# Moving the residual's multiplications by gamma from GpSimd to VectorE in a two-layer transformer trunk

## The chip, the cores and the metric

The kernel runs on one core of a Trainium2 chip. The metric is the device time of one execution in microseconds (us). A core has a matrix engine (TensorE, PE in the profile; its loads of stationary operands are PEld), VectorE (DVE), ScalarE (ACT), GpSimd (POOL) and SyncE (SP), which issues DMAs. Each engine works through its own list of instructions in order, and waits at an instruction until what it needs is there.

## The reference

The trunk has two layers over 256 tokens with 2048 channels, in float32. Layer 0 mixes tokens by gated linear attention (GLA), layer 1 by a neighbourhood attention (16 heads), and each mixer is followed by a gated feed-forward block of 5632 channels with a convolution of width 3 ("FFN"). Behind each of the four sub-layers stands

```
x = layer_norm(alpha * x + f(x), gamma, beta)
# layer_norm: (x - mean) * rsqrt(var + 1e-5) * gamma + beta, over the 2048 channels
```

so there are four normalizations: behind GLA, FFN 0, attention and FFN 1. The first three ("mid") feed another sub-layer, the last gives the output.

## The kernel before

**Matmuls.** float32 is emulated: each operand x is split into `hi` (a rounded copy, ScalarE, line 131) and `lo` = x - `hi` (VectorE, line 132), and three products hi·hi, hi·lo, lo·hi are added in PSUM. The weights (416 units of 1 MB) come by DMA into `raw`, are split in two halves each, and wait in four pairs of buffers. So VectorE makes two `lo` halves of 128x1024 for every unit, all through the program.

**Layout.** The residual stream lies in `x_sb`, two tiles of 128 tokens (t = 0, 1) by 2048 channels. The activations that feed the matmuls are held transposed and split, in `xT` (input of a sub-layer) and `gT` (its inner result). A sub-layer's last matmul (`residual_out`) gives blocks of 128x512; VectorE adds them into `x_sb` (lines 365, 367) and takes statistics (line 371). For the last block, t = 0 is finished first and then t = 1, and the next sub-layer's first block of matmuls is written the same way ("apart"): 48 matmuls (16 chunks of channels, three products each) that read `xT` of t = 0, then 48 that read t = 1.

**A mid normalization** (`ln_mid`, line 287) is, for each t:
- head: mean and variance (`ln_mv`, line 282); variance + epsilon (`rs_m`, line 274) and its power -1/2 (`ln_rs`, line 275), both on GpSimd; then four 128x512 pieces (x - mean)·rstd in place on VectorE (line 293);
- turn, four times: four TensorE transposes of a 512-wide block of `x_sb` (line 299) into one of three PSUM buffers `ps_tp`; gamma and beta per channel by ScalarE (line 307) and VectorE (line 309) in turns; then the split into `xT` (lines 131, 132);
- resid (line 312): `x_sb` itself, for the next residual sum, is multiplied by gamma in four 128x512 pieces on GpSimd (line 315, gamma in the tile `g`, copied to all partitions), and beta is added by an accumulating DMA (line 316).

**Order.** The code is written in the order of PE's work. Small steps are put into a list (`later`) with a due time in "ticks" (a tick is called every few matmuls). The order on each engine that results is not the written order: a scheduler places instructions by priority (written order, shifted by offsets for the splits and the turns) and by when it expects their inputs.

**Pools.** `gb`, the tile of gamma, lies in the pool of the stage (ffn0, ffn1). In the attention stage the tiles `bt` (bias, loaded by two GpSimd DMAs at lines 706 and 707), `qk` and `pt` have two buffers each.

Of the kernel before, what the change touches and what calls it, by code (L numbers as in the profile page):

```python
# [17 lines left out]
P = 128  # L18
# [58 lines left out]
def kernel(  # L77
# [92 lines left out]

    side = []

# [98 lines left out]
    def rsqrt(dst, src, scale, eps, small):  # L271

        m = small.tile([P, 1], F32, tag="rs_m", name="rs_m", bufs=2)
        nc.gpsimd.tensor_scalar(m, src, scale, eps, ALU.mult, ALU.add)  # L274
        nc.gpsimd.tensor_tensor(dst, m, mhalf, ALU.pow)  # L275
# [11 lines left out]
    def ln_mid(pool, xs, t, stats, idx, gb):  # L287
# [23 lines left out]

        def resid():
            for b in range(4):
                sl = slice(b * 512, b * 512 + 512)
                nc.gpsimd.tensor_tensor(xs[:, t, sl], xs[:, t, sl], gb[:, sl], ALU.mult)
            nc.gpsimd.dma_start(xs[:, t], lnp[idx, 1:2, :].broadcast_to([P, D]), accum_op=ALU.add)

        later(head, 0)
        for b, n in enumerate((4, 0, 0, 0)):
            later(lambda b=b: turn(b), n)  # L320
        later(resid, 0)

    def ln_last(pool, xs, t, stats, gb):
        def go():
            mv, rstd = ln_head(pool, xs, t, stats)
            nmr = pool.tile([P, 1], F32, tag="ln_nm", name="ln_nm", bufs=2)
            nc.vector.scalar_tensor_tensor(nmr, mv[:, 0:1], -1.0, rstd, ALU.mult, ALU.mult)
            for b in (3, 0, 1, 2):
                sl = slice(b * 512, b * 512 + 512)
                blk = xs[:, t, sl]  # L330
                if b == 3:
                    nc.scalar.activation(blk, blk, AF.Identity, bias=nmr, scale=rstd)
                    nc.gpsimd.tensor_tensor(blk, blk, gb[:, 0, sl], ALU.mult)
                    nc.gpsimd.tensor_tensor(blk, blk, gb[:, 1, sl], ALU.add)
                else:
                    nc.vector.scalar_tensor_tensor(blk, blk, mv[:, 0:1], gb[:, 0, sl], ALU.subtract, ALU.mult)  # L336
                    nc.vector.scalar_tensor_tensor(blk, blk, rstd, gb[:, 1, sl], ALU.mult, ALU.add)  # L337
                (nc.scalar if b == 3 else nc.sync).dma_start(out[t * P:t * P + P, sl], blk)
        later(go, 0)
# [6 lines left out]
    def load_gb(pool, idx):  # L346
        gb = pool.tile([P, 2, D], F32, tag="gb", name="gb")
        for i in range(2):
            nc.gpsimd.dma_start(gb[:, i], lnp[idx, i:i + 1, :].broadcast_to([P, D]))
        return gb  # L350

    def residual_out(act_in, first, last, n, idx, begin=None):
# [3 lines left out]
        for nb in range(4):  # L356
            def evac(t, ps):
                if begin is not None and not cell:
                    begin()
                    cell["begun"] = True  # L360
                pool, xs, gb = scope["pool"], scope["x"], scope["gb"]
                sl = slice(nb * 512, nb * 512 + 512)
                blk = xs[:, t, sl]
                if first:
                    nc.vector.scalar_tensor_tensor(blk, blk, ALPHA, ps, ALU.mult, ALU.add)  # L365
                else:
                    nc.vector.tensor_tensor(blk, ps, blk, ALU.add)  # L367
                if last:
                    if t not in stats:
                        stats[t] = pool.tile([P, 4, 6], F32, tag="ln_st", name="ln_st", bufs=2)  # L370
                    nc.vector.bn_stats(stats[t][:, nb], blk)  # L371
                    if nb == 3:
                        if idx == 2 * DEPTH - 1:
                            ln_last(pool, xs, t, stats[t], gb)
                        else:
                            ln_mid(pool, xs, t, stats[t], idx, gb)
            as_block(act_in, n, evac, apart=last and nb == 3, settle=nb == 0)
# [250 lines left out]
    def ffn(layer):  # L628
# [23 lines left out]
        for part, (c0, n) in enumerate(THIRDS):  # L652
# [39 lines left out]
            if part == 0:  # L692
                scope["gb"] = (load_gb if idx == 2 * DEPTH - 1 else load_g)(pool, idx)
            residual_out(gT, part == 0, part == len(THIRDS) - 1, n // 4, idx)


    def attention():
# [3 lines left out]
        def head(h):  # L701
            pool = scope["pool"]
            q = pool.tile([P, 2, T], F32R, tag="q", name="q", bufs=2)
            k = pool.tile([P, 2, T], F32R, tag="k", name="k", bufs=2)
            bt = pool.tile([P, 6, GW], F32, tag="bt", name="bt", bufs=2)
            nc.gpsimd.dma_start(bt, bias[h])
# [3 lines left out]
            def qk_out(dst, ps):  # L710
                f = pool.tile([P, T], F32, tag="qk", name="qk", bufs=2)
                join(pool, f, ps)
# [29 lines left out]
            def turn():  # L742
                s = cell["s"]
                tp = ps_tp()
                for kt in range(2):
                    for i in range(2):
                        nc.tensor.transpose(tp[:, kt * T + i * P:kt * T + i * P + P],
                                            s[:, i, kt * P:kt * P + P], ident)
                pt = pool.tile([P, 2, 512], F32R, tag="pt", name="pt", bufs=2)
                cell["pt"] = pt.rearrange("p h (k n) -> p h k n", k=2)  # L750
# [33 lines left out]
    def begin_gla_out():  # L784
# [5 lines left out]
        nc.gpsimd.dma_start(scope["x"], x.rearrange("(t p) d -> p t d", p=P))  # L790
        scope["gb"] = load_g(open_pool("ffn0"), 0)

    def begin_na_out():
        scope["gb"] = load_g(swap_pool("ffn1"), 2)

# [79 lines left out]
```

## Time and profile before

| what | value |
|---|---|
| median of three runs | 2297.3 us (2296.99 to 2300.06) |
| the profiled execution's own time | 2300.88 us |
| its span, first to last instruction | 2299.2 us |
| PE busy | 2265.1 us (99%) |
| VectorE busy | 1511.0 us (66%) |
| ScalarE busy | 1053.2 us (46%) |
| GpSimd busy | 371.1 us (16%) |
| line 315, the 24 multiplications on GpSimd | 44.4 us |

The busy time of an engine is an average over all stages. An engine with a share of 99% can still be held up in a few places, and an engine with 66% can be the one that is waited for in one stretch. The profiled execution took 3.6 us more than the median.

### The profile page before, as it was taken

The page shows a single profiled execution, that of the slowest core. Times are in us where ns is not written, and L with a number is a line of the kernel's source. Part 1 is how long each engine was busy: PE and PEld are TensorE (multiplying, and loading weights), DVE is VectorE, ACT ScalarE, POOL GpSimd, SP SyncE. Part 2 cuts the span into 40 slices and gives each one's busy share as a digit, 9 for nine tenths or more (in the row PEclk, how much of TensorE's full clock was granted, in tenths as well). Part 3 has the DMA queues.
Part 4 walks back from the last instruction along what each step waited for, and adds up shares of the span by engine and source line. Part 5 has one row for each costly group of instructions (what it writes and reads, how often), then busy time and mean ns, then how long its engine had stood idle before and what let it go on. Part 6 is the DMA issues. An engine that isn't in the chain of part 4 may idle for free. (4 is left out here: it accounts for less than half of the span.)

```text
span 2299.2 us, 29601 instructions
## 1 busy us (share of the span) xinstructions
PE 2265.1 (99%) x11728; PEld 1923.9 (84%) x11728; DVE 1511.0 (66%) x2053; ACT 1053.2 (46%) x1529; POOL 371.1 (16%) x312
## 2 busy tenths in 40 slices
PE   8999999999999999999999999999999999999997
PEld 7888888788888888888778888878888888888886
DVE  6656656867656675576676666667776567656775
ACT  6554543544434444344355555445444344434442
POOL 1111001222102220122120000022220022201211
PEclk9999999999999999999999999999999999999999
DMA  7444464644555556555585555556556555555452
GB/s 277 174 177 167 181 241 151 235 183 182 206 197 181 176 177 217 183 184 183 183 241 189 193 185 194 197 169 236 182 182 220 185 182 183 183 211 190 176 193 92
DMA packets 66604, 439.03 MB, mean 191 GB/s; under 512 B 7649, under 2 KB 9697, under 8 KB 15137
## 3 DMA queue, kind: packets, MB, share of 16 engines
q1 hardware_dynamic: 60336, 415.00, 50.3%
q0 software_dynamic: 5840, 21.61, 3.7%
q8 instruction: 92, 1.51, 0.3%
q10 hardware_dynamic: 288, 0.52, 0.1%
q14 instruction: 48, 0.39, 0.0%
HBM read 431.87 MB, written 2.10 MB: 189 GB/s over the span
## 5 line engine op out<-in xcount | busy, mean ns | idle before, releaser
L132 DVE TENSOR_TENSOR lo<-raw,hi 128x1024 fp32r<-128x1024 f32 (+1 forms) x793 | 950.6, 1217 | 502.1 <-ACT hi L131 500.8
L190 PE MATMUL ps_mm<-xT,hi 128*128 128x512 f32 x3472 | 1232.6, 399 | 6.4 <-ACT hi L131 6.1
L131 ACT CAST hi<-raw 128x1024 fp32r<-128x1024 f32 (+1 forms) x793 | 807.9, 1040 | 526.8 <-PE ps_mm L190 480.4
L190 PE MATMUL ps_mm<-xT,lo 128*128 128x256 f32 x3472 | 976.5, 281 | 0.3 <-DVE lo L132 0.3
L190 PEld LDWEIGHTS ps_mm<-xT,hi 128*128 128x128 f32 x3472 | 653.4, 188 | 167.2 <-ACT hi L131 6.1
L190 PEld LDWEIGHTS ps_mm<-xT,lo 128*128 128x128 f32 x3472 | 657.1, 189 | 2.1 <-DVE lo L132 1.5
L190 PE MATMUL ps_mm<-hi,gT 128*128 128x512 f32 x1920 | 594.7, 389 | 0.0
L190 PEld LDWEIGHTS ps_mm<-hi,gT 128*128 128x128 f32 x1920 | 360.4, 188 | 75.0
L647 POOL TENSOR_SCALAR c<-h,cw,cb 128x256 f32<-128x256 f32 x168 | 239.9, 1428 | 1101.6 <-DVE h L466 1101.6
L190 PE MATMUL ps_mm<-lo,gT 128*128 128x512 f32 x960 | 373.8, 389 | 0.0
L190 PE MATMUL ps_mm<-hi,xT 128*128 128x512 f32 x896 | 286.0, 393 | 1.7 <-DVE xT L132 1.7
L190 PEld LDWEIGHTS ps_mm<-lo,gT 128*128 128x128 f32 x960 | 180.2, 188 | 36.8
L190 PEld LDWEIGHTS ps_mm<-hi,xT 128*128 128x128 f32 x896 | 168.1, 188 | 37.7 <-DVE xT L132 3.5
L190 PE MATMUL ps_mm<-lo,xT 128*128 128x512 f32 x448 | 175.2, 391 | 2.9 <-DVE lo L132 2.9
L131 ACT CAST gT<-gg 128x256 fp32r<-128x256 f32 x88 | 35.6, 407 | 288.5 <-DVE gg L665 288.5
L660 ACT ACTIVATE ge<-c 128x256 f32<-128x256 f32 x88 | 36.8, 418 | 253.4 <-DVE c L649 253.4
L648 DVE SCALAR_TENSOR_TENSOR c<-h,cw,c 128x255 f32<-128x255 f32 x168 | 81.3, 484 | 76.8 <-POOL c L647 76.8
L190 PEld LDWEIGHTS ps_mm<-lo,xT 128*128 128x128 f32 x448 | 84.4, 189 | 20.9 <-DVE lo L132 4.4
L649 DVE SCALAR_TENSOR_TENSOR c<-h,cw,c 128x255 f32<-128x255 f32 x168 | 81.3, 484 | 5.9
L465 ACT COPY join_t<-ps_mm 128x256 f32<-128x256 f32 x216 | 78.3, 363 | 0.0
L466 DVE TENSOR_TENSOR h<-ps_mm,join_t 128x256 f32<-128x256 f32 x168 | 70.2, 418 | 0.0
L132 DVE TENSOR_TENSOR gT<-gg,gT 128x256 fp32r<-128x256 f32 x88 | 37.7, 430 | 38.8 <-ACT gT L131 38.8
(132 smaller groups left out, 818.8 us busy)
## 6 DMA issues: line engine op xcount, KB each, us to landing
raw<-in_w_dram SPq DMA_DIRECT2D x388, 1024.0 KB, 4.8
x_sb<-in_lnp_dram POOLq DMA_DIRECT2D x6, 1024.0 KB, 9.9
raw<-in_w_dram SPq DMA_DIRECT2D x16, 256.0 KB, 5.5
g<-in_lnp_dram POOLq DMA_DIRECT2D x3, 1024.0 KB, 13.6
bt<-in_bias_dram POOLq DMA_DIRECT2D x16, 192.0 KB, 2.8
bt<-bmask_sb POOLq DMA_DIRECT2D x16, 192.0 KB, 3.0
xr<-in_xt_dram SPq DMA_DIRECT2D x8, 256.0 KB, 5.6
x_sb<-in_x_dram POOLq DMA_DIRECT2D x1, 2048.0 KB, 9.6
```

The lines of the kernel that those rows point to most:

```text
L131: nc.scalar.copy(hi, src)
L132: nc.vector.tensor_tensor(lo, src, hi.bitcast(F32), ALU.subtract)
L190: nc.tensor.matmul(o, l, r, start=start, stop=stop)
L465: nc.scalar.copy(tmp, ps4[:, :, 1])
L466: nc.vector.tensor_tensor(dst.rearrange("p (t n) -> p t n", t=2), ps4[:, :, 0], tmp, ALU.add)
L647: nc.gpsimd.tensor_scalar(c, hh, w_[:, 1:2], cb[:, ch:ch + 1], ALU.mult, ALU.add)
L648: nc.vector.scalar_tensor_tensor(c[:, 1:], hh[:, :T - 1], w_[:, 0:1], c[:, 1:], ALU.mult, ALU.add)
L649: nc.vector.scalar_tensor_tensor(c[:, :T - 1], hh[:, 1:], w_[:, 2:3], c[:, :T - 1], ALU.mult, ALU.add)
L660: nc.scalar.activation(ge, c, AF.Gelu)
```

## The change

1. `resid` is cut into four steps, one for each 512-wide piece, that multiply on VectorE. They go into a new list `slow`, with due times 36, 44, 52 and 60 ticks behind the normalization's end; a tick takes at most one of them. The accumulating DMA stays on GpSimd's queue, behind the fourth piece.
2. `rs_m` (variance plus epsilon) goes from GpSimd to VectorE, in all the normalizations, GLA's included; the power stays on GpSimd.
3. Gamma's tile goes into the pool of `x_sb`, which lives to the end, and `load_gb` for the last normalization takes gamma from there and beta from a tile `b` of its own.
4. `bt`, `qk` and `pt` in the attention stage have one buffer in place of two.

```diff
-    side = []
+    side, slow = [], []
...
         while side and side[0][0] <= st["tick"]:
             side.pop(0)[1]()
+
+        if slow and slow[0][0] <= st["tick"]:
+            slow.pop(0)[1]()
...
         m = small.tile([P, 1], F32, tag="rs_m", name="rs_m", bufs=2)
-        nc.gpsimd.tensor_scalar(m, src, scale, eps, ALU.mult, ALU.add)
+        nc.vector.tensor_scalar(m, src, scale, eps, ALU.mult, ALU.add)
         nc.gpsimd.tensor_tensor(dst, m, mhalf, ALU.pow)
...
-        def resid():
-            for b in range(4):
-                sl = slice(b * 512, b * 512 + 512)
-                nc.gpsimd.tensor_tensor(xs[:, t, sl], xs[:, t, sl], gb[:, sl], ALU.mult)
-            nc.gpsimd.dma_start(xs[:, t], lnp[idx, 1:2, :].broadcast_to([P, D]), accum_op=ALU.add)
+        def resid(b):
+            sl = slice(b * 512, b * 512 + 512)
+            nc.vector.tensor_tensor(xs[:, t, sl], xs[:, t, sl], gb[:, sl], ALU.mult)
+            if b == 3:
+                nc.gpsimd.dma_start(xs[:, t], lnp[idx, 1:2, :].broadcast_to([P, D]), accum_op=ALU.add)
...
-        later(resid, 0)
+        for b in range(4):
+            slow.append((st["tick"] + 36 + 8 * b, lambda b=b: resid(b)))
...
     def load_gb(pool, idx):
-        gb = pool.tile([P, 2, D], F32, tag="gb", name="gb")
-        for i in range(2):
-            nc.gpsimd.dma_start(gb[:, i], lnp[idx, i:i + 1, :].broadcast_to([P, D]))
-        return gb
+        b = pool.tile([P, D], F32, tag="b", name="b")
+        nc.gpsimd.dma_start(b, lnp[idx, 1:2, :].broadcast_to([P, D]))
+        return load_g(scope["xp"], idx), b
...
-            bt = pool.tile([P, 6, GW], F32, tag="bt", name="bt", bufs=2)
+            bt = pool.tile([P, 6, GW], F32, tag="bt", name="bt", bufs=1)
...
-                f = pool.tile([P, T], F32, tag="qk", name="qk", bufs=2)
+                f = pool.tile([P, T], F32, tag="qk", name="qk", bufs=1)
...
-                pt = pool.tile([P, 2, 512], F32R, tag="pt", name="pt", bufs=2)
+                pt = pool.tile([P, 2, 512], F32R, tag="pt", name="pt", bufs=1)
```

What this does to the order on an engine can be read from the built program. In the rows below, a row is a line of the kernel, the operation, out<-in and the shape, and x4 means four of it in a row. The changed kernel's lines are 3 to 4 higher: there 277 is `rs_m`, 285 `ln_mv`, 296 the normalization (293 before), 302 the transposes (299), 312 gamma and beta for `xT` (309), 317 the multiplication of the residual by gamma (315), and 369 and 375 the sum and the statistics (365 and 371).

**First place: VectorE in the first normalization, behind the head of t = 0.** Before:

```order
L293 TENSOR_SCALAR x_sb<-x_sb,ln_mv,ln_rs 128x512 x4
L132 TENSOR_TENSOR lo<-raw,hi 128x1024 x2
L309 TENSOR_SCALAR ln_f<-ps_tp,lng_sb 128x128 x3
L132 TENSOR_TENSOR lo<-raw,hi 128x1024
L132 TENSOR_TENSOR xT<-ln_f,xT 128x4x128
L309 TENSOR_SCALAR ln_f<-ps_tp,lng_sb 128x128
L132 TENSOR_TENSOR lo<-raw,hi 128x1024
L309 TENSOR_SCALAR ln_f<-ps_tp,lng_sb 128x128
```

and with the change:

```order
L277 TENSOR_SCALAR rs_m<-ln_mv 128x1
L296 TENSOR_SCALAR x_sb<-x_sb,ln_mv,ln_rs 128x512 x4
L132 TENSOR_TENSOR lo<-raw,hi 128x1024 x2
L312 TENSOR_SCALAR ln_f<-ps_tp,lng_sb 128x128 x2
L317 TENSOR_TENSOR x_sb<-x_sb,g 128x512
L312 TENSOR_SCALAR ln_f<-ps_tp,lng_sb 128x128
L317 TENSOR_TENSOR x_sb<-x_sb,g 128x512
L312 TENSOR_SCALAR ln_f<-ps_tp,lng_sb 128x128
L132 TENSOR_TENSOR lo<-raw,hi 128x1024
L132 TENSOR_TENSOR xT<-ln_f,xT 128x4x128 x2
L132 TENSOR_TENSOR lo<-raw,hi 128x1024
```

The first two multiplications of t = 0 by gamma (line 317) stand right behind the first turns, and not some 36 ticks further on; `rs_m` stands in front of the head's four pieces.

**Second place: VectorE a little further on, around the head of t = 1.** Before:

```order
L132 TENSOR_TENSOR xT<-ln_f,xT 128x4x128
L282 BN_AGGR ln_mv<-ln_st 128x2
L132 TENSOR_TENSOR lo<-raw,hi 128x1024
L309 TENSOR_SCALAR ln_f<-ps_tp,lng_sb 128x128
L293 TENSOR_SCALAR x_sb<-x_sb,ln_mv,ln_rs 128x512 x2
L132 TENSOR_TENSOR xT<-ln_f,xT 128x4x128
L293 TENSOR_SCALAR x_sb<-x_sb,ln_mv,ln_rs 128x512
L309 TENSOR_SCALAR ln_f<-ps_tp,lng_sb 128x128
L293 TENSOR_SCALAR x_sb<-x_sb,ln_mv,ln_rs 128x512
L309 TENSOR_SCALAR ln_f<-ps_tp,lng_sb 128x128 x2
```

and with the change:

```order
L132 TENSOR_TENSOR lo<-raw,hi 128x1024
L132 TENSOR_TENSOR xT<-ln_f,xT 128x4x128 x2
L285 BN_AGGR ln_mv<-ln_st 128x2
L132 TENSOR_TENSOR lo<-raw,hi 128x1024
L277 TENSOR_SCALAR rs_m<-ln_mv 128x1
L132 TENSOR_TENSOR lo<-raw,hi 128x1024
L296 TENSOR_SCALAR x_sb<-x_sb,ln_mv,ln_rs 128x512 x4
L312 TENSOR_SCALAR ln_f<-ps_tp,lng_sb 128x128
L132 TENSOR_TENSOR lo<-raw,hi 128x1024
L312 TENSOR_SCALAR ln_f<-ps_tp,lng_sb 128x128 x2
L317 TENSOR_TENSOR x_sb<-x_sb,g 128x512
L132 TENSOR_TENSOR xT<-ln_f,xT 128x4x128
```

One more `lo` half stands between `ln_mv` and the head's pieces, with `rs_m` in the middle; the four pieces now follow on each other; and one multiplication follows each pair or so of line 312, six of the eight of both t before the last `xT`.

**Third place: PE at the same head of t = 1.** `hi` and `lo` rows are matmuls of the next stage that read `xT` of t = 0. Before:

```order
L190 MATMUL ps_mm<-lo,xT 128x512
L190 MATMUL ps_mm<-hi,xT 128x512
L299 MATMUL ps_tp<-ident,x_sb 128x128 x8
L190 MATMUL ps_mm<-hi,xT 128x512
L190 MATMUL ps_mm<-lo,xT 128x512
L190 MATMUL ps_mm<-hi,xT 128x512
L299 MATMUL ps_tp<-ident,x_sb 128x128 x4
```

and with the change:

```order
L193 MATMUL ps_mm<-hi,xT 128x512 x2
L193 MATMUL ps_mm<-lo,xT 128x512
L193 MATMUL ps_mm<-hi,xT 128x512 x2
L193 MATMUL ps_mm<-lo,xT 128x512
L193 MATMUL ps_mm<-hi,xT 128x512 x2
L193 MATMUL ps_mm<-lo,xT 128x512
L193 MATMUL ps_mm<-hi,xT 128x512
L302 MATMUL ps_tp<-ident,x_sb 128x128 x12
L193 MATMUL ps_mm<-hi,xT 128x512
```

PE does 9 more matmuls before it comes to the transposes of t = 1, and takes three turns' transposes at once there. The other two mid normalizations show the same pattern (in the second, 6 more matmuls), and behind them the order on PE, VectorE and ScalarE is the one of before.

## Rows read from the trace of the kernel before

**Rows 1.** Waits of PE, whole program: who waited for whom: us, times, longest.

```profile
PE ps_tp L299 <- DVE x_sb L293: 6.3, 4, 2.4
...
PE ps_mm L190 <- DVE lo L132: 3.3, 4, 1.3
...
PE ps_mm L190 <- DVE xT L132: 2.0, 3, 0.9
```

**Rows 2.** Busy times in 2 us stretches: PE, PEld, DVE, ACT, POOL, then PE's granted clock.

```profile
408.00:410.00 2.00, 2.00 (x9) 1.56 (x8) 2.00 (x4) 0.83 (x3) 2.00 (x2) 0.50 1.01 356
...
1550.00:1552.00 2.00, 1.29 (x10) 0.85 (x8) 2.00 (x4) 0.83 (x3) 2.00 (x2) 1.00 1.03 356
```

**Rows 3.** Timeline, first normalization: start us, us, engine, line, x, [idle before <- releaser].

```profile
387.50 0.19 POOL L274 TENSOR_SCALAR rs_m<-ln_mv 128x1 f32<-128x1 f32 x1 [72.29 <-DVE ln_mv L282]
...
388.37 1.91 DVE L293 TENSOR_SCALAR x_sb<-x_sb,ln_mv,ln_rs 128x512 f32<-128x512 f32 x4 [0.96 <-POOL ln_rs L275]
...
390.26 8.63 POOL L315 TENSOR_TENSOR x_sb<-x_sb,g 128x512 f32<-128x512 f32 x4 [1.93 <-PE ps_tp L299]
...
394.34 1.70 DVE L132 TENSOR_TENSOR lo<-raw,hi 128x1024 fp32r<-128x1024 f32 x1 [0.53 <-ACT hi L131]
...
395.96 1.78 DVE L132 TENSOR_TENSOR xT<-ln_f,xT 128x512 fp32r<-128x512 f32 x1
...
397.98 2.00 DVE L132 TENSOR_TENSOR lo<-raw,hi 128x1024 fp32r<-128x1024 f32 x1
...
398.94 0.39 PE L190 MATMUL ps_mm<-hi,xT 128*128 128x512 f32 x1
...
399.90 0.40 DVE L309 TENSOR_SCALAR ln_f<-ps_tp,lng_sb 128x128 f32<-128x128 f32 x1
...
401.36 0.68 DVE L132 TENSOR_TENSOR xT<-ln_f,xT 128x512 fp32r<-128x512 f32 x1
...
404.56 1.15 DVE L132 TENSOR_TENSOR lo<-raw,hi 128x1024 fp32r<-128x1024 f32 x1
...
404.74 1.02 POOL L274 TENSOR_SCALAR rs_m<-ln_mv 128x1 f32<-128x1 f32 x1 [4.59 <-DVE ln_mv L282]
...
405.84 0.57 POOL L275 TENSOR_TENSOR ln_rs<-rs_m,mhalf 128x1 f32<-128x1 f32 x1
...
406.45 1.00 DVE L293 TENSOR_SCALAR x_sb<-x_sb,ln_mv,ln_rs 128x512 f32<-128x512 f32 x2 [0.42 <-POOL ln_rs L275]
...
407.05 1.63 PE L299 MATMUL ps_tp<-ident,x_sb 128*128 128x128 f32 x8 [2.40 <-DVE x_sb L293]
...
417.29 0.40 PE L190 MATMUL ps_mm<-lo,xT 128*128 128x512 f32 x1
```

**Rows 4.** Timeline of the second and third normalization.

```profile
1146.93 0.40 PE L190 MATMUL ps_mm<-hi,xT 128*128 128x512 f32 x1
...
1155.74 1.00 DVE L293 TENSOR_SCALAR x_sb<-x_sb,ln_mv,ln_rs 128x512 f32<-128x512 f32 x2
...
1164.17 0.61 PE L190 MATMUL ps_mm<-hi,xT 128*128 128x512 f32 x2
...
1540.98 0.39 PE L190 MATMUL ps_mm<-hi,xT 128*128 128x512 f32 x1
...
1559.12 0.40 PE L190 MATMUL ps_mm<-lo,xT 128*128 128x512 f32 x1
```

**Rows 5.** Timeline, the end of the program, first token tile.

```profile
2279.26 0.75 DVE L336 SCALAR_TENSOR_TENSOR x_sb<-x_sb,ln_mv,gb 128x512 f32<-128x512 f32 x1
...
2279.31 0.75 POOL L274 TENSOR_SCALAR rs_m<-ln_mv 128x1 f32<-128x1 f32 x1 [50.65 <-DVE ln_mv L282]
...
2280.73 0.16 DVE L327 SCALAR_TENSOR_TENSOR ln_nm<-ln_mv,ln_rs 128x1 f32<-128x1 f32 x1 [0.73 <-POOL ln_rs L275]
```

**Rows 6.** Timeline of GpSimd in the attention stage: the loads of `bt`.

```profile
1193.04 0.56 POOL L706 DMA_DIRECT2D bt<-in_bias_dram  x1 [16.69 <-DVE s L729]
...
1206.30 0.57 POOL L706 DMA_DIRECT2D bt<-in_bias_dram  x1 [7.61 <-DVE s L729]
```

More of the change, by code (lines that the diff above doesn't have):

```diff
@@ L332, in go @@
                     nc.scalar.activation(blk, blk, AF.Identity, bias=nmr, scale=rstd)
-                    nc.gpsimd.tensor_tensor(blk, blk, gb[:, 0, sl], ALU.mult)
-                    nc.gpsimd.tensor_tensor(blk, blk, gb[:, 1, sl], ALU.add)
-                else:
-                    nc.vector.scalar_tensor_tensor(blk, blk, mv[:, 0:1], gb[:, 0, sl], ALU.subtract, ALU.mult)
-                    nc.vector.scalar_tensor_tensor(blk, blk, rstd, gb[:, 1, sl], ALU.mult, ALU.add)
+                    nc.gpsimd.tensor_tensor(blk, blk, gb[0][:, sl], ALU.mult)
+                    nc.gpsimd.tensor_tensor(blk, blk, gb[1][:, sl], ALU.add)
+                else:
+                    nc.vector.scalar_tensor_tensor(blk, blk, mv[:, 0:1], gb[0][:, sl], ALU.subtract, ALU.mult)
+                    nc.vector.scalar_tensor_tensor(blk, blk, rstd, gb[1][:, sl], ALU.mult, ALU.add)
                 (nc.scalar if b == 3 else nc.sync).dma_start(out[t * P:t * P + P, sl], blk)
@@ L360, in evac @@
                     cell["begun"] = True
-                pool, xs, gb = scope["pool"], scope["x"], scope["gb"]
+                assert not (first and nb == 0 and slow)
+                pool, xs = scope["pool"], scope["x"]
                 sl = slice(nb * 512, nb * 512 + 512)
@@ L373, in evac @@
                         if idx == 2 * DEPTH - 1:
-                            ln_last(pool, xs, t, stats[t], gb)
+                            ln_last(pool, xs, t, stats[t], scope["gb"])
                         else:
-                            ln_mid(pool, xs, t, stats[t], idx, gb)
+                            ln_mid(pool, xs, t, stats[t], idx, scope["gb"])
             as_block(act_in, n, evac, apart=last and nb == 3, settle=nb == 0)
@@ L692, in ffn @@
             if part == 0:
-                scope["gb"] = (load_gb if idx == 2 * DEPTH - 1 else load_g)(pool, idx)
+                scope["gb"] = load_gb(pool, idx) if idx == 2 * DEPTH - 1 else load_g(scope["xp"], idx)
             residual_out(gT, part == 0, part == len(THIRDS) - 1, n // 4, idx)
@@ L790, in begin_gla_out @@
         nc.gpsimd.dma_start(scope["x"], x.rearrange("(t p) d -> p t d", p=P))
-        scope["gb"] = load_g(open_pool("ffn0"), 0)
+        scope["xp"] = xp
+        scope["gb"] = load_g(xp, 0)
+        open_pool("ffn0")
     def begin_na_out():
-        scope["gb"] = load_g(swap_pool("ffn1"), 2)
+        swap_pool("ffn1")
+        scope["gb"] = load_g(scope["xp"], 2)
     residual_out(gT, True, True, 4, 0, begin_gla_out)
```

## The prediction

> **What bounds the kernel now.** I read the page first: PE is busy for 2265.1 of 2299.2 us, so all that a change of the other engines can give back are PE's idle stretches, and I asked for its list of waits next. There one kind of place fills the top [rows 1]: PE waits 6.3 us for the normalized pieces of `x_sb` (line 293), 3.3 us for `lo` halves and 2.0 us for `xT`, and every one of these releasers is VectorE. Nearly all of it lies in the three mid normalizations. In one of them PE's granted clock was 0.50, the 1.2 GHz level, behind an idle stretch of 2.40 us, in another it stayed at 1.00 [rows 2]; both stretches took the same time within 0.2 us (below), so I give the clock no term of its own.
>
> The timeline of the first normalization [rows 3] shows why VectorE is late. The head of t = 0 is done by 390.28. GpSimd then multiplies by gamma for 8.63 us, and in just this time VectorE's work swells: a `lo` half takes 1.70 and 2.00 us, where one behind it takes 1.15, and an `xT` piece 1.78, where the later one takes 0.68. VectorE is then hardly free until the head of t = 1 starts at 406.45, while PE has run dry at 404.65 (its next start, 407.05, less 2.40). The turns of t = 1 go the same way. From the first matmul on `xT` (398.94) to the 48th (417.29, so to 417.5) 18.6 us pass; 48 matmuls at the 0.23 us that 24 of them take up to 404.65 are 11.0, and 16 transposes some 2. In the third normalization it is 1540.98 to 1559.12, 18.4 us, in the second 1146.93 to 1164.17, and 2 matmuls, 17.7 us [rows 4].
>
> **The multiplications.** The change takes 24 of them from GpSimd, 2.16 us each by the first four [rows 3], and GpSimd's time is worth nothing in itself. It adds 24 to VectorE. No such row exists; the nearest, an operation on two tensors in SBUF of the same shape, is `xT` with 0.68 us [rows 3]. I take that. The bounds are nothing (if each falls into a wait) and the 1.78 of the crowded row. They do not run "36 ticks on": the order puts two of t = 0 in front of the head of t = 1, and four more among the turns of t = 1. So VectorE, the engine that PE waits for, gets more work in this very stretch, and loses the slowing by GpSimd in exchange.
>
> **Epsilon.** `rs_m` on VectorE: `ln_nm` on the same shape took 0.16 us [rows 5]; bounds 0 and, from the row of `rs_m` on GpSimd that had no neighbour, 0.19 [rows 3]. What matters more is what stands beside the power, which stays on GpSimd. In the first normalization `rs_m` started at 404.74 beside a `lo` that had begun at 404.56, and ended at 405.76, 0.05 behind that `lo`; alone it took 0.19 [rows 3]. The power will now start beside the next `lo`, so I let it wait for that `lo`'s end and add its 0.57: between nothing and 0.6 us later for each head of t = 1. The Trainium skill (SBUF — State Buffer, section "Who interferes with whom") has the rule: VectorE instructions with two SBUF inputs and GpSimd instructions that read SBUF take a shared port pair as an exclusive lock, for a whole instruction, and the later one blocks. It speaks for the multiplications' move and against this one. By the rule and by the row the head is late by those 0.6 us; without either, the sum below would be 1.8 us larger.
>
> **VectorE in the first normalization, step by step.** From the head of t = 0 (388.37, some 0.1 earlier with `rs_m` on VectorE) to the head of t = 1 the new order has four pieces (4 x 0.48), seven `lo` (7 x 1.15), eight of line 309 (8 x 0.40, the row at 399.90), four `xT` and two multiplications (6 x 0.68), the sum and the statistics of t = 1 (2 x 0.68), `ln_mv` and `rs_m` (2 x 0.16): 18.9 us. The same sum over the old order (six `lo`, three `xT`, no multiplication, no `rs_m`) is 15.6. The old stretch took 18.1; the swelling in the three crowded rows (0.55 + 1.10 + 0.85) and the waits in the rows (0.53 and 0.42) would make it 19.1, so instructions overlap by some 1.0. With that overlap, 0.7 of waits for ScalarE's steps (an estimate, from the 0.53 of before and one more, shorter) and 0.6 for the power, the new stretch is 19.2, and the head of t = 1 starts at 407.5, **1.0 later** than before.
>
> That would be a loss, if PE came at the same time. But it does 9 more matmuls first (2.1 us) and, since the fourth turn of t = 0 now waits behind one multiplication, is itself 0.3 late: it arrives at 407.0. The first piece is ready at 408.0, so PE waits 1.0 in place of 2.4. The three turns end with the third piece and its four transposes, at 409.5. Then come the other 15 matmuls (3.4), one turn (0.5) and perhaps 0.4 of waiting for a `ps_tp`: 413.8 in place of 417.5. In t = 1 the four `xT` come 0.7 to 3 us ahead of PE by the same prices, and so do the `lo` halves. **The first normalization gives 3.7 us**, the third by the same order 18.4 - 14.9 = **3.5**.
>
> In the second, only 36 matmuls of t = 1 stand in front (48 in the others), so there is less cover. Its head of t = 1 goes from 1155.74 [rows 4] to some 1157.2 by the same additions, PE waits about 1 us for the third `xT` and 1 for the head, and ends at 1162.8 in place of 1164.6: **1.8**.
>
> **The end of the program.** `rs_m` took 0.75 us there, beside line 336, which took the same 0.75 [rows 5]. Without it the power would still meet line 336, which VectorE issues right behind `rs_m`, so I take 0.1 for each of the two tiles, **0.2** together; the bounds are 0 and 2 x 0.6.
>
> **What costs nothing.** `rs_m` in GLA: PE's waits name nothing there [rows 1], four units of split weights cover VectorE, and without that cover it would be eight times the 0.57 of a power. Gamma's tile: its load waits for the multiplications that read the last one, and both are done long before the next normalization. The accumulating DMA starts later, with the rest of an FFN third (or the attention) to land in; if that were too short, the next residual sum would wait. The single buffers in attention: `bt` of the next head is loaded once the scores of this head are done, as 1193.04 shows, and the next scores come 13.3 us later, at 1206.30; the two DMAs are issued by 1198.7 (1206.30 less 7.61) [rows 6], so the second has 7.6 us to land. If it were late, VectorE would wait for it, 16 times. `qk` and `pt` are written again a unit of weights and a head later, and the order on PE, VectorE and ScalarE there is the old one.
>
> **The sum**: 3.7 + 1.8 + 3.5 + 0.2 = 9.2 us. Against the profiled execution's own 2300.88 us this gives 2291.7. That execution is 3.6 above the median of the three runs, so the forecast for the median is 2297.3 - 9.2 = **2288.1 us**. A measurement of this kernel can tell some 0.2%, 4.6 us, from no change.
>
> **Rivals.**
> - *All of it comes back.* If the power slips in ahead of the `lo` and the scheduler's order fits the real times, PE does not wait at all: the 11.6 us of [rows 1] and up to 1.2 at the end, near 13: 2284.5. For it: the new order takes the heads' pieces in one go, and PE later. Against: VectorE's own sum above is longer than before. Chance 0.15.
> - *The wait only changes its name.* PE waits for `xT` of t = 1, behind the multiplications, in place of line 293. Each normalization keeps all but about 1 us: 2294. For it: VectorE has no gap from 394 to 406 now, and gets 8 x 0.68 more. Against: the slowing it loses is 2.5 us in the first half alone. Chance 0.18.
> - *Slower.* If VectorE's operations swell for another reason than GpSimd (the turns' traffic itself), nothing is given back, and the head of t = 1 is late by two multiplications, a `lo` and the power, 3.3 us, of which PE's 9 matmuls cover 2.1; the four multiplications behind it push `xT` by 2.7, which 15 matmuls mostly cover. Some 2 us in each normalization: 2303. It decides at the `lo` beside the first turns: from 1.6 us up with GpSimd idle, this is the case. Against it: a `lo` at 404.56 in the same stretch took 1.15, with GpSimd's multiplications over. Chance 0.07.
> - That the change does not do what it says is settled by the order: the multiplications are not "well into the next stage". Had they been, VectorE would be free of 6 x 0.68 us in the stretch.
>
> **How the numbers follow.** The forecast has a chance of 0.60. With all mechanisms' bounds (the power 1.8 in sum, the end of the program 1.0, the `xT` waits of the second normalization about 2) it spans 2285.5 to 2291; to leave out no more than 2 in 10 the range goes on to 2283 and 2294. Faster by over 0.2% are the forecast and the first rival, with a little of the second: 0.77; within 0.2% is most of the second, 0.16; slower 0.07.
>
> **What would show it.** Right: no GpSimd multiplication beside `lo` and `xT`, each `lo` at 1.15 to 1.25; line 293 of t = 1 in four pieces of about 0.5, starting 0 to 1.5 us later than before against the first `xT` matmul; PE's wait there near 1 us; the power ending some 0.6 behind a `lo`; the multiplications near 0.68; PE's three groups of waits at 5 us or less in place of 11.6. Wrong: `lo` still swollen, PE's waits for `xT` grown, or a new wait in attention for `bt`.

## The result, and the profile after

The changed kernel takes **2284.6 us** (median of 5 runs, 2284.36 to 2284.88). The runs of before that go with it have a median of 2299.8 us (5 runs, 2296.99 to 2300.06); the ratio is 0.9935, with a 95% interval of 0.9925 to 0.9946. That is 15.2 us faster, where the forecast was 9.2 us from a base of 2297.3. The time lies inside the stated range (2283 to 2294), 3.5 us under the forecast of 2288.1 and just outside the 2285.5 to 2291 that the mechanisms' own bounds gave. The profiled executions differ by 16.3 us (span 2299.2 before, 2282.9 after), and the rest of this section accounts for these 16.3.

Busy time of the engines after (busy us, share of the span, instructions):

```profile
PE 2260.0 (99%) x11728; PEld 1923.6 (84%) x11728; DVE 1509.9 (66%) x2093; ACT 1053.7 (46%) x1529; POOL 321.9 (14%) x272
```

VectorE has 40 instructions more, 24 of them the multiplications, and is busy for 1.1 us less than the 1511.0 of before: what it gained in work it lost in swelling. PE does the same work and is "busy" for 5.1 us less than the 2265.1 of before, to which we come back. PE's list of waits after (us in total, times, longest), against [rows 1]:

```profile
PE ps_mm L193 <- ACT hi L131: 6.1, 1, 6.1
PE ps_tp L302 <- DVE ln_f L312: 1.5, 3, 0.5
PE ps_mm L193 <- DVE xT L132: 1.1, 3, 0.5
PE ps_mm L193 <- DVE lo L132: 0.7, 1, 0.7
PE ps_tp L302 <- DVE x_sb L296: 0.2, 1, 0.2
```

The first line is the start of the program, as before. The 6.3 us for `x_sb` have become 0.2, the 3.3 for `lo` 0.7. The timeline of the first normalization after (start, duration, engine, line, operation; in brackets the idle time before it and its releaser), against [rows 3]:

```profile
387.29 1.92 DVE L296 TENSOR_SCALAR x_sb<-x_sb,ln_mv,ln_rs 128x512 f32<-128x512 f32 x4 [0.68 <-POOL ln_rs L278]
...
392.03 0.68 DVE L317 TENSOR_TENSOR x_sb<-x_sb,g 128x512 f32<-128x512 f32 x1
...
393.95 1.22 DVE L132 TENSOR_TENSOR lo<-raw,hi 128x1024 fp32r<-128x1024 f32 x1
395.08 1.29 DVE L132 TENSOR_TENSOR xT<-ln_f,xT 128x512 fp32r<-128x512 f32 x2
...
397.92 0.39 PE L193 MATMUL ps_mm<-hi,xT 128*128 128x512 f32 x1
...
403.54 0.14 DVE L277 TENSOR_SCALAR rs_m<-ln_mv 128x1 f32<-128x1 f32 x1
403.60 1.21 DVE L132 TENSOR_TENSOR lo<-raw,hi 128x1024 fp32r<-128x1024 f32 x1
403.77 1.46 POOL L278 TENSOR_TENSOR ln_rs<-rs_m,mhalf 128x1 f32<-128x1 f32 x1 [16.51 <-DVE rs_m L277]
405.26 1.91 DVE L296 TENSOR_SCALAR x_sb<-x_sb,ln_mv,ln_rs 128x512 f32<-128x512 f32 x4 [0.45 <-POOL ln_rs L278]
...
405.87 1.57 PE L302 MATMUL ps_tp<-ident,x_sb 128*128 128x128 f32 x12
...
410.95 0.62 PE L193 MATMUL ps_mm<-hi,xT 128*128 128x512 f32 x2
```

A `lo` takes 1.22 where it took 1.70 and 2.00, an `xT` piece 0.65 where it took 1.78. The head of t = 1 starts at 405.26, 17.97 us behind the head of t = 0 (before 18.08), and PE arrives at it without a wait in its own list (the weight load of its first transpose waits 0.5 us), having done 33 matmuls on `xT` first (24 before). The last row holds the 48th matmul: 13.3 us after the first one (to 411.2), where it was 18.6.

**Where the 16.3 us are.** PE's list lost 10.8 us (14.3 to 3.5 without the start). The list of waits of PE's weight loads (PEld) shows more. Before:

```profile
PEld ps_mm L190 <- ACT hi L131: 6.1, 1, 6.1
PEld ps_mm L190 <- DVE lo L132: 6.0, 7, 1.7
PEld ps_tp L299 <- DVE x_sb L293: 5.9, 3, 2.8
PEld ps_mm L190 <- DVE xT L132: 4.3, 6, 1.4
PEld ps_tp L299 <- DVE ln_f L309: 3.9, 5, 0.9
PEld ps_tp L299 <- ACT ln_f L307: 2.6, 3, 1.2
PEld ps_tp L190 <- ACT sh L131: 0.9, 1, 0.9
PEld ps_tp L681 <- ACT ht L675: 0.8, 1, 0.8
```

and after:

```profile
PEld ps_mm L193 <- ACT hi L131: 6.1, 1, 6.1
PEld ps_tp L302 <- DVE ln_f L312: 3.1, 5, 0.9
PEld ps_mm L193 <- DVE xT L132: 2.8, 4, 1.0
PEld ps_mm L193 <- DVE lo L132: 1.9, 3, 1.1
PEld ps_tp L302 <- DVE x_sb L296: 1.6, 3, 0.7
PEld ps_mm L193 <- DVE rs_m L277: 0.7, 2, 0.4
PEld ps_tp L193 <- DVE sl L132: 0.2, 1, 0.2
```

Without the first row these are 25.2 us before (0.8 of it in rows not shown) and 10.3 after: 14.9 less. Beside them stands the clock. Before, three 2-us windows of the first normalization have a granted clock below 1 (0.89, 0.50, 0.75 from 406 to 412, the middle one in [rows 2]), and 2 us times what is missing in each is 1.72. After, every window but those of the first and last 20 us shows 1.00. Together 16.6, against 16.3 measured. The two belong to one account and are not two prices: what the low clock took in that normalization, PE would else have spent waiting, as the second profile of the kernel before shows (`before_again`). PE's own list falls short, it seems, because part of a wait for weights is shown as a busy matmul, and because matmuls at the low clock are busy for longer: the work is the same 11728 instructions, and 5.1 us of "busy" went. The Trainium skill (Perfetto Trace Analysis, section "Tensor Engine Instruction (MATMUL, LD_WEIGHTS)") has a reason that fits: a matmul's end is estimated in the profile, not observed.

By stage, each from one start of `ln_mv` for t = 0 to the next (the first from the program's start, the last to its end), in us:

| kernel | GLA | 1st norm., FFN 0 | 2nd norm., attention | 3rd norm., FFN 1 | end |
|---|---|---|---|---|---|
| before | 387.1 | 750.7 | 391.3 | 749.8 | 20.2 |
| after | 386.2 | 744.6 | 387.8 | 744.6 | 19.8 |
| gain (forecast) | 1.0 (0) | 6.2 (3.7) | 3.6 (1.8) | 5.2 (3.5) | 0.4 (0.2) |

Counted in the two traces from one of PE's matmuls to the same one, the gain of these three stages lies in the normalizations themselves (6.1, 3.5 and 5.2 us); in the rest of them the two kernels run alike within 0.1 us.

### The profile page after: what moved, and what is told of

It is laid out like the page before. It is cut to its first block, busy times and chain, and to the rows that moved or that the text cites. A ratio compares the mean times of both kernels' runs of the same rounds, so it can differ in the third digit from the quotient of the medians.

```text
span 2282.9 us, 29599 instructions
## 1 busy us (share of the span) xinstructions
PE 2260.0 (99%) x11728; PEld 1923.6 (84%) x11728; DVE 1509.9 (66%) x2093; ACT 1053.7 (46%) x1529; POOL 321.9 (14%) x272
## 4 chain that ended last, share of the span: by engine, by line
PE 40%; DVE 4%; issue 3%; POOL 2%; ACT 1%; ACTq 0%; POOLq 0%
PE ps_mm L193 38%; DVE lo L132 2%; POOL c L651 2%; ACT hi L131 1%; PE ps_tp L193 1%; DVE c L653 0%; DVE c L652 0%; DVE h L470 0%; PE ps_tp L751 0%; DVE gg L669 0%; POOL ln_rs L278 0%; PE ps_tp L302 0%; DVE x_sb L341 0%; DVE x_sb L296 0%; DVE xT L132 0%
## 6 DMA issues: line engine op xcount, KB each, us to landing
g<-in_lnp_dram POOLq DMA_DIRECT2D x4, 1024.0 KB, 14.7
```

## The experiments

Two theories stood at first. **A**: GpSimd's multiplications slowed VectorE in the normalizations; moving them is nearly all of the gain, and VectorE has room for them. **B**: the gain comes from `rs_m` leaving GpSimd and from the order that this gives PE. **C** is a variant of A: the moved multiplications still cost VectorE what the forecast said. The stages of every profile, and their balance, come first, to be looked up from the runs below ("loads' waits" are PEld's without those for `hi` that the start makes; "clock" is the loss as above; "rest" is the span less these and less the waits for `hi`). In `ghost`, `twice` and `late_on_pool` the clock falls before PE's wait is over, so 0.7, 1.2 and 0.7 us of their "clock" stand in the waits as well:

| kernel | GLA | 1st, FFN 0 | 2nd, attention | 3rd, FFN 1 | end | loads' waits | clock | rest |
|---|---|---|---|---|---|---|---|---|
| before | 387.1 | 750.7 | 391.3 | 749.8 | 20.2 | 25.2 | 1.7 | 2266.2 |
| before_again | 388.5 | 750.7 | 391.3 | 746.6 | 20.2 | 26.2 | 1.7 | 2263.0 |
| after | 386.2 | 744.6 | 387.8 | 744.6 | 19.8 | 10.3 | 0 | 2266.5 |
| mults_only | 385.8 | 745.7 | 389.0 | 745.6 | 20.2 | 12.7 | 0 | 2267.3 |
| eps_only | 387.2 | 750.0 | 388.8 | 748.5 | 19.8 | 18.3 | 3.4 | 2266.5 |
| ghost | 385.9 | 754.2 | 395.4 | 744.6 | 19.8 | 22.6 | 5.1 | 2265.9 |
| no_mult | 386.0 | 744.9 | 386.5 | 744.9 | 19.8 | 8.2 | 0 | 2267.7 |
| really_late | 385.8 | 744.9 | 387.0 | 744.9 | 19.8 | 8.6 | 0 | 2267.1 |
| late_on_pool | 385.8 | 744.9 | 397.4 | 744.9 | 19.8 | 16.4 | 3.4 | 2266.7 |
| twice | 385.8 | 744.4 | 395.3 | 744.4 | 19.7 | 13.8 | 3.4 | 2266.4 |
| twice_ffn | 387.1 | 744.4 | 387.8 | 744.4 | 19.8 | 10.4 | 0 | 2267.2 |
| late_on_pool_ffn | 385.2 | 744.9 | 387.8 | 744.9 | 20.1 | 8.9 | 0 | 2267.3 |

### mults_only: the multiplications move, epsilon stays

```diff
-        nc.vector.tensor_scalar(m, src, scale, eps, ALU.mult, ALU.add)
+        nc.gpsimd.tensor_scalar(m, src, scale, eps, ALU.mult, ALU.add)
```

> The changed kernel with rs_m back on GpSimd; the multiplications stay on VectorE. Theory A (GpSimd's multiplications slowed VectorE in the normalizations, and moving them is nearly all of the gain): 2286 to 2288.5 us, no lo above 1.3 us in the first turns; what is lost against 2284.6 are the 1.0 us of GLA (PE waits 0.5 us for sh again, the first normalization's ln_mv starts at about 387.1) and up to 0.5 us in each normalization and at the end, where rs_m waits beside lo. Theory B (the gain comes from rs_m leaving GpSimd and from the order that this gives PE): 2293 to 2299 us.

Measured 2288.3 us (2287.12 to 2290.67), ratio 0.9948 (0.9936 to 0.9961). Theory A's number, and B falls: the three normalization stages give 5.0, 2.3 and 4.2 us of the changed kernel's 6.2, 3.6 and 5.2. One part of A's expectation is wrong: GLA's gain is there (385.8), so it does not come from `rs_m`. In attention PE waited 1.5 us behind a weight load that landed late, and this is all that the second stage lacks: its normalization is 0.4 us shorter than the changed kernel's (from `ln_mv` of t = 0 to the same late matmul on `xT` 1131.48 to 1164.73, there 1130.73 to 1164.36).

### eps_only: epsilon moves, the multiplications stay

```diff
-        nc.gpsimd.tensor_scalar(m, src, scale, eps, ALU.mult, ALU.add)
+        nc.vector.tensor_scalar(m, src, scale, eps, ALU.mult, ALU.add)
```

> The kernel before with rs_m on VectorE; the multiplications stay on GpSimd. Theory A: 2294.5 to 2298.5 us, lo at 1.7 to 2.0 us beside GpSimd's multiplications, PE's wait for the pieces of x_sb of t = 1 still 2 us or more in the first and third normalization; ln_mv of the first normalization at about 386.2 (the 1.0 us of GLA). Theory B: 2291 us or less, and that wait below 1 us.

Measured 2293.5 us (2293.03 to 2296.1), ratio 0.9972 (0.9961 to 0.9982), which is 6.8 us under the 2300.3 of its runs of before and 1 us below A's expectation: `rs_m` is worth more than A said, in the second normalization above all (2.5 us). But the swelling stays, as its VectorE timeline shows:

```profile
394.35 1.69 DVE L132 TENSOR_TENSOR lo<-raw,hi 128x1024 fp32r<-128x1024 f32 x1 [0.52 <-ACT hi L131]
395.97 1.77 DVE L132 TENSOR_TENSOR xT<-ln_f,xT 128x512 fp32r<-128x512 f32 x1
...
407.76 2.89 DVE L293 TENSOR_SCALAR x_sb<-x_sb,ln_mv,ln_rs 128x512 f32<-128x512 f32 x4
```

The longest wait of PE behind the start is 1.9 us, and the clock falls in two normalizations (3.4 us). The profiled execution was the slowest of the seven (2296.1), so its stages show less of the gain than the median. The two halves alone give 11.9 and 6.8 against these runs, 18.7 in sum, and both together 15.2 against their own. Part of the gain may be had by either, but the intervals (9.0 to 14.7, 4.1 to 9.0 and 12.4 to 17.2) do not settle it.

### ghost: the changed kernel, with GpSimd's multiplications added for nothing

```diff
+        def ghost():
+            for b in range(4):
+                sl = slice(b * 512, b * 512 + 512)
+                scr = pool.tile([P, 512], F32, tag="scr", name="scr")
+                nc.gpsimd.tensor_tensor(scr, xs[:, t, sl], gb[:, sl], ALU.mult)
...
+        if idx < 2:
+            later(ghost, 0)
```

> The changed kernel, and GpSimd again multiplies x_sb by gamma at the old place, four pieces per tile, but into a scratch tile that nobody reads, in the first and second normalization only; the order on TensorE, VectorE and ScalarE is that of the changed kernel, instruction by instruction. Theory A: lo at 1.6 to 2.0 us and xT up to 1.8 us beside these multiplications in the first two normalizations, the head of t = 1 some 2 to 2.5 us later against its ln_mv of t = 0, PE waits 2 us or more there in each; the third normalization as in the changed kernel; in all 2289 to 2293 us. The rival (VectorE's operations swelled from the traffic of the turns themselves, or GpSimd's multiplications cost nothing and the new order is the gain): 2284 to 2285.5 us, the three normalizations alike.

Measured 2301.95 us (2301.06 to 2303.85), ratio 1.0008 (0.9999 to 1.0017): with sixteen useless multiplications on an engine that nobody waits for, the whole gain is gone. The first stage is 9.6 us longer than in the changed kernel, the second 7.6, and the third, which has no ghost, 744.6 as there. The order on TensorE, VectorE and ScalarE is the changed kernel's, and in these normalizations VectorE waits for GpSimd only for the power, as there. So the cause is that GpSimd's multiplications slow VectorE's operations beside them. The loss is more than expected; a likely reason is that the ghost need not wait for the transposes and starts beside the head's pieces, not behind them. VectorE's and GpSimd's timeline:

```profile
387.08 3.86 DVE L296 TENSOR_SCALAR x_sb<-x_sb,ln_mv,ln_rs 128x512 f32<-128x512 f32 x4 [0.68 <-POOL ln_rs L278]
390.86 4.51 DVE L132 TENSOR_TENSOR lo<-raw,hi 128x1024 fp32r<-128x1024 f32 x2
```

```profile
387.71 6.58 POOL L325 TENSOR_TENSOR scr<-x_sb,g 128x512 f32<-128x512 f32 x4 [0.67 <-DVE x_sb L296]
```

The four pieces take 3.86 us (1.92 in the changed kernel), the two `lo` 4.51 (2.35). PE waits 4.2 us in one go, and its clock is granted at half for some 6 us behind that. The Trainium skill (SBUF — State Buffer, "Who interferes with whom") counts `tensor_scalar` in a two-port mode among the instructions that take the shared ports, beside those with two inputs in SBUF; the swelling of the pieces of line 296, of one tensor input, agrees, though no row shows in which mode they run.

### no_mult and really_late: what room VectorE has

`no_mult` leaves line 317 out:

```diff
-            nc.vector.tensor_tensor(xs[:, t, sl], xs[:, t, sl], gb[:, sl], ALU.mult)
```

`really_late` ties each multiplication to a weight half that is in use at its tick, which the scheduler can't bring forward:

```diff
+            one = scope["pool"].tile([P, 1], F32, tag="rs_m", name="one", bufs=2)
+            nc.vector.tensor_scalar(one, st["lo"][:, 0:1].bitcast(F32), 0.0, 1.0, ALU.mult, ALU.add)
-            nc.vector.tensor_tensor(xs[:, t, sl], xs[:, t, sl], gb[:, sl], ALU.mult)
+            nc.vector.scalar_tensor_tensor(xs[:, t, sl], xs[:, t, sl], one, gb[:, sl], ALU.mult, ALU.mult)
```

> The changed kernel with the residual's multiplications by gamma left out altogether (the residual is the normalized x plus beta, without gamma). Theory A with cover (VectorE has room for the 24 multiplications; the forecast's sum over VectorE was too large): 2283.5 to 2285 us, what is left in PE's waits is the 0.5 us per normalization for ln_f. Theory C (the multiplications still cost what the forecast's sum held, about 1 us of PE's waiting in each normalization): 2281 to 2282.5 us.

> The changed kernel with the multiplications really late: each now also multiplies by a 1 that VectorE forms from the weights' lo half in use at that tick, so the order has all four of a tile behind its normalization, in the next stage. If the early multiplications lie in VectorE's cover (theory A): 2283 to 2285.5 us, no faster than no_mult's 2283.9 by more than 0.5; PEld's waits without the one at the start stay at 8 to 11 us. If they still cost their share of VectorE in the normalization (theory C): 2281 to 2282.5 us, PEld's waits below 7 us.

Measured 2283.9 us (2283.55 to 2285.4; ratio 0.9929, 0.9917 to 0.9942) and 2284.6 us (2284.35 to 2286.06; 0.9939, 0.9927 to 0.9952). Theory C falls for the whole: leaving the multiplications out wins 0.7 us, which these runs can hardly tell from nothing, and having them later wins nothing, though in the changed kernel six of the eight of each normalization sit in its crowded stretch. By stage it holds in one place. The first and third are 0.3 us longer without the multiplications, but the second is 1.3 us shorter (386.5, against the 387.8 that three profiles with them there share), and 0.8 shorter with them later. So in front of attention, where the forecast saw less cover, they still cost about 1 us.

`no_mult` and `eps_only` together give the price of GpSimd's multiplications at their own place. The two traces have the same order on TensorE, VectorE and ScalarE in the mid normalizations, instruction by instruction; `eps_only` adds the multiplications on GpSimd. The rows of `no_mult`, against those of `eps_only` above:

```profile
393.07 1.23 DVE L132 TENSOR_TENSOR lo<-raw,hi 128x1024 fp32r<-128x1024 f32 x1 [0.52 <-ACT hi L131]
394.21 0.69 DVE L132 TENSOR_TENSOR xT<-ln_f,xT 128x512 fp32r<-128x512 f32 x1
...
404.36 1.91 DVE L296 TENSOR_SCALAR x_sb<-x_sb,ln_mv,ln_rs 128x512 f32<-128x512 f32 x4
```

The medians are 9.6 us apart, the three stages of the profiles 5.1, 2.3 and 3.6. So against the runs of before in this set, `rs_m` with the order that comes with it gives 6.8 us, and taking GpSimd's multiplications out of the way another 9.6.

### twice and late_on_pool: a wait in another place

`twice` writes each multiplication two times:

```diff
             nc.vector.tensor_tensor(xs[:, t, sl], xs[:, t, sl], gb[:, sl], ALU.mult)
+            nc.vector.tensor_tensor(xs[:, t, sl], xs[:, t, sl], gb[:, sl], ALU.mult)
```

`late_on_pool` has the late places of `really_late` and GpSimd as the engine:

```diff
-            nc.vector.scalar_tensor_tensor(xs[:, t, sl], xs[:, t, sl], one, gb[:, sl], ALU.mult, ALU.mult)
+            nc.gpsimd.tensor_tensor(gb[:, b * 512:b * 512 + 1], gb[:, b * 512:b * 512 + 1], one, ALU.mult)
+            nc.gpsimd.tensor_tensor(xs[:, t, sl], xs[:, t, sl], gb[:, sl], ALU.mult)
```

> The changed kernel with each multiplication on VectorE done two times (the residual gets gamma squared). In the changed kernel the first piece of t = 1 is ready 0.13 us before PE's transposes start, and two multiplications stand ahead of it, so two more (1.2 us at 0.6 apiece) make PE wait some 1.1 us in the first and third normalization, and a little less for xT of t = 1; together 2287 to 2290 us. If VectorE has more to spare than the trace shows: 2286 us or less. If the multiplications cost like on GpSimd: 2293 us or more.

> The same late places, but the multiplications on GpSimd (a tiny one by the 1 ahead of each holds them back; rs_m stays on VectorE). Theory A, in the form that GpSimd's multiplications hurt only where VectorE has no time to spare: 2283 to 2286.5 us, although the multiplications swell lo beside them just the same (1.6 us and more), because four units of split weights stand in front of PE there. The rival, that GpSimd's multiplications beside VectorE cost time wherever they stand: 2290 us or more.

Measured 2291.6 us (2290.88 to 2293.15; ratio 0.9967, 0.9955 to 0.9978) and 2295.1 us (2293.74 to 2296.9; 0.9985, 0.9976 to 0.9994). The first is above its expectation, and the second is the rival's number: read as totals, both would speak for a price of the multiplications themselves. The stages say otherwise: first and third are as fast as in the changed kernel, and 7.5 and 9.6 us are lost in the second. GpSimd's and VectorE's timelines of `twice`, in attention:

```profile
1180.95 0.87 POOL L320 DMA_DIRECT2D x_sb<-in_lnp_dram  x1 [12.39 <-PE ps_tp L193]
1182.04 0.56 POOL L711 DMA_DIRECT2D bt<-in_bias_dram  x1 [0.22 <-issue]
1182.59 0.55 POOL L348 DMA_DIRECT2D g<-in_lnp_dram  x1
1192.83 0.90 POOL L712 DMA_DIRECT2D bt<-bmask_sb  x1 [9.69 <-DMA bt<-in_bias_dram]
```

```profile
1201.36 0.76 DVE L734 SCALAR_TENSOR_TENSOR s<-ps_tp,bt 128x256 f32<-128x256 f32 x2 [8.48 <-DMA bt<-bmask_sb]
```

The accumulating DMA and the load of the next gamma (1 MB each) are issued around `bt`'s first DMA. Its second can be issued only 10.8 us after the first and lands 8.5 us after VectorE wants it; PE stands for 5.3 us, and the clock falls to half some 2.4 us before PE goes on:

```profile
1200.00:1202.00 2.00, 0.00 (x0) 0.00 (x0) 0.64 (x2) 0.00 (x0) 0.00 (x0) 1.00 0.04 9
1202.00:1204.00 2.00, 0.00 (x0) 0.00 (x0) 1.94 (x4) 1.13 (x5) 0.56 (x1) 0.67 0.22 37
1204.00:1206.00 2.00, 0.91 (x5) 0.93 (x6) 1.91 (x5) 1.47 (x3) 0.64 (x1) 0.50 0.16 61
1206.00:1208.00 2.00, 2.00 (x8) 1.71 (x8) 1.45 (x3) 0.59 (x1) 0.23 (x1) 0.50 0.70 98
1208.00:1210.00 2.00, 2.00 (x9) 1.71 (x9) 0.37 (x1) 1.44 (x3) 0.00 (x0) 0.63 0.92 345
```

(The columns are the window, its length, the busy time of PE, PEld, DVE, ACT and POOL, the granted clock, the DMA engines' share, GB/s.) In `late_on_pool` VectorE waits 9.5 us for `bt`, PE 6.3; there, three of the multiplications stand in GpSimd's list between `bt`'s two DMAs as well.

### twice_ffn and late_on_pool_ffn: the same without that wait

Both have the edit for the first and third normalization only; the second is as in the changed kernel. For `twice_ffn` (`late_on_pool_ffn` branches in the same way):

```diff
             nc.vector.tensor_tensor(xs[:, t, sl], xs[:, t, sl], gb[:, sl], ALU.mult)
+            if idx != 1:
+                nc.vector.tensor_tensor(xs[:, t, sl], xs[:, t, sl], gb[:, sl], ALU.mult)
```

> As the run that does each multiplication two times, but only in the first and third normalization (their residual gets gamma squared); the second, in front of attention, has each once. The profile of that run puts its loss at one place: PE waits 5.3 us in attention for the scores of the second head, whose bt lands late behind the accumulating DMAs and gamma's load, and the clock is granted at half for some 7 us behind it. If that is all: 2283.5 to 2286 us, as the changed kernel, no PE wait over 1 us, no granted clock below 1. If the doubled multiplications themselves cost time in VectorE's order: 2288 us or more.

> As the run with the multiplications really late on GpSimd, but only for the first and third normalization; the second has them on VectorE as in the changed kernel. If that run's loss was the late bt alone (its PE wait of 6.3 us and the clock behind it): 2283.5 to 2286.5 us, although lo beside these multiplications swells to 1.6 us and more; then GpSimd's multiplications cost nothing where VectorE has time to spare, and the change could have moved them in time instead of to another engine. If they cost time wherever they stand: 2289 us or more.

Measured 2285.0 us (2284.39 to 2285.2; ratio 0.9936, 0.9923 to 0.9948) and 2285.7 us (2284.65 to 2286.13; 0.9939, 0.9925 to 0.9952): both within 1.1 us of the changed kernel, with stages of 744.4 and 744.9 against 744.6. So sixteen more multiplications on VectorE cost nothing that can be told, and neither do sixteen on GpSimd, once they lie where VectorE is ahead. They swell `lo` there too, from 1.22 to 2.29 us, and nobody waits. The timelines of `late_on_pool_ffn`:

```profile
458.29 2.56 POOL L324 TENSOR_TENSOR x_sb<-x_sb,g 128x512 f32<-128x512 f32 x2
```

```profile
459.63 2.29 DVE L132 TENSOR_TENSOR lo<-raw,hi 128x1024 fp32r<-128x1024 f32 x1 [1.49 <-ACT hi L131]
462.18 1.21 DVE L132 TENSOR_TENSOR lo<-raw,hi 128x1024 fp32r<-128x1024 f32 x1
```

### before_again: does the balance hold?

No edit: the kernel before, profiled a second time.

> The kernel before once more, for a second profile of it. If PEld's waits and the lost clock together make up the time: its span less that of the changed kernel (2282.9) equals the difference of PEld's waits plus the clock's loss (the sum over 2-us windows of 2 us times one less the granted clock) within 1 us, as it does in the first profile (14.6 and 1.7 against 16.3). If not, a rest of 2 us or more stays.

One run, 2299.04 us, span 2297.3. The expectation is missed: its loads' waits and clock exceed the changed kernel's by 17.6 us, the span by 14.4, a rest of 3.2. In the other eleven profiles the rest lies between 2265.9 and 2267.7, so the balance is good to about 1 us in general, and not always. The missing 3 us have a place: between 1580 and 1720 us, behind the third normalization, PE does 117 or 118 matmuls in 20 us where the first profile has 115, busy throughout and at a granted clock of 1.00 in both. One window of the first profile, then the same of the second:

```profile
1620.00:1640.00 20.00, 20.00 (x115) 1.00 0.56 197
```

```profile
1620.00:1640.00 20.00, 20.00 (x117) 1.00 0.47 167
```

Why PE was quicker there stays open.

The second profile also shows what the low clock costs in the kernel before, for this time it fell in the third normalization, and in the first it stayed at 1.00:

```profile
408.38 1.17 PE L299 MATMUL ps_tp<-ident,x_sb 128*128 128x128 f32 x8 [2.40 <-DVE x_sb L293]
...
417.66 0.50 PE L190 MATMUL ps_mm<-lo,xT 128*128 128x512 f32 x1 [1.27 <-DVE lo L132]
```

From these transposes to that matmul 9.28 us pass, and at the low clock of the first profile 9.43 (407.05 in [rows 3] to 416.48). In the third normalization it is 9.27 at the full clock and 9.08 at the low one. The loads' waits make up for it: 5.8 us in the first normalization at the low clock, 7.5 at the full one. So the low clock cost nothing here beyond 0.2 us: PE was waiting for VectorE anyway.

## Why the prediction was right, and where its sizes were off

**Right: the mechanism.** GpSimd's multiplications made VectorE late, and without them VectorE's operations have their own lengths (`lo` 1.22, `xT` 0.65, the multiplication 0.68, `rs_m` 0.14 against the 0.16 taken). `ghost`, and `eps_only` beside `no_mult`, show the cause by themselves. The slower rival needed a `lo` of 1.6 us with GpSimd idle: in the whole changed kernel none takes over 1.23. The rival in which the wait changes its name to `xT` is out too: 1.1 us over the whole program.

**The term that was mis-sized: VectorE's stretch in a normalization.** The sum of its rows was right (18.9 forecast, 18.96 in the rows after, a merged row counted as it stands). But instructions overlap by 1.44 us, where 1.0 was taken; VectorE never waits for ScalarE in the stretch, where 0.7 was set; and the power costs 0.45 in place of 0.6. So it took 17.97, not 19.2, and the head of t = 1 came 0.2 us earlier than before against the head of t = 0's statistics, not 1.0 later. PE's wait there is 0 in its own list and 0.5 in its loads' (2.4 and 2.8 before), not 1.0, and the 48 matmuls take 13.3 us, not 14.9. Another 0.8 us came behind them, at the transposes of line 681, for which PE no longer waits; the forecast had no term for these. The third normalization is alike: 1530.28 to 1543.5, 13.2 us (18.4 before, 14.9 forecast). In the second the stretch takes 14.1 us (17.7 before, 15.9 forecast): PE waits 0.4 us for `xT` and 0.2 for the head, where about 1 was set for each.

**Luck.** This is, in effect, the rival "all of it comes back", given a chance of 0.15, though not by its condition: the power did not slip in ahead of the `lo`. That its time, 2284.5, was met within 0.1 is luck. It was a gain of 12.8 us from 2297.3; the measured gain is 15.2 from 2299.8. From that base the forecast would have been 2290.6, 6 us above the measured time.

**The ceiling was too low.** The prediction took PE's idle stretches for all that can come back, and that rival put the ceiling near 13 us, from PE's list of waits. The loads' list and the clock had 26.9 us to give back, of which 16.6 went. To give the clock no term of its own was right: each of the two normalizations took the same time within 0.2 us with and without the low clock (`before_again`).

**Epsilon.** The forecast expected the power to be blocked behind a `lo`, and it was: 1.46 us beside a `lo` in place of 0.57 in [rows 3], released 0.42 behind that `lo`'s end. It counted that as a loss of 0.6 in each normalization. In two of the three the runs say the move is a gain: without it the first and third stage are 1.1 and 1.0 us longer (`mults_only`), the end of the program 0.4. In the second the 1.3 us are attention's late weight load, and the normalization itself is 0.4 us shorter without the move. PE's order changes with it (27 matmuls on `xT` in front of the transposes of t = 1 in the first normalization of `mults_only`, 33 in the changed kernel), and which of the two, order or wait, makes the difference was not taken apart.

**What costs nothing.** GLA gained 1.0 us, forecast as nothing. It takes 385.2 to 387.1 us in the profiles of the changed kernel and of those built on it, and 387.1 to 388.5 in the three others (`before` two times, `eps_only`); `rs_m` is not its cause (`mults_only`, `eps_only`), and the cause stays open. For `bt`'s single buffer the forecast counted 7.6 us of room for its second DMA. PE indeed never waits in the changed kernel, but it is closer than that: VectorE does wait, once.

```profile
DVE s L733 <- DMA bt<-bmask_sb: 2.0, 1, 2.0
```

The room was counted from attention's steady state, without the two 1 MB DMAs on the same queue; `twice` and `late_on_pool` show the cost when it runs out.

## What to carry to other kernels

Work on an engine that nobody waits for is not free beside the engine that is waited for: here four multiplications per tile, 8.6 us of GpSimd's time for the first tile, cost 2 to 5 us in each normalization (`eps_only` against `no_mult`), and the same work cost nothing some 30 to 60 us later in the first and third (`late_on_pool_ffn`). Before moving such work to the busier engine, see whether it can move in time; and when it moves, check what stands behind it on the DMA queue. Take the ceiling of a gain from the waits of the weight loads, with the low clock beside them, and not from PE's list alone. And compare stage by stage: `twice` and `late_on_pool` would have been misread by their totals.

## What was not expected of the hardware

- The granted clock can fall at a wait of PE. In six profiles it goes to 0.50, the 1.2 GHz level, between 2.4 us before PE goes on (`twice`) and 1.1 us behind that (`eps_only`), and 1.7 to 5.1 us of clock are missing: the two of `before` (longest wait 2.40 us), `eps_only` (1.9), `ghost` (4.2), `twice` (5.3) and `late_on_pool` (6.3). In the six others, where PE waits for 1.5 us at most, it stays at 1.00. It is not every long wait: of the two of 2.40 us in `before`, one was followed by it.
- What the low clock costs depends on what PE meets next: nothing beyond 0.2 us in `before`, where PE has to wait for VectorE again, and some 2.2 us in `twice` (half of the 4.4 us from PE's restart to 1209.5), whose second stage is 7.5 us longer than the changed kernel's with a wait of 5.3.
- The changed kernel's five runs lie within 0.5 us, those of before in a range of 3 us here and of 7.7 us over all runs (2295.12 to 2302.81). Its mean granted clock is 0.998 in each, that of before between 0.996 and 0.998.
- GpSimd's contention reaches VectorE's `tensor_scalar` with one tensor input: 3.86 us for four pieces in place of 1.92.
